# Product-key experts in a two-block transformer: gate products for 128 first indices at once, half of them kept in DRAM

## The chip, the cores and the metric

The kernel runs on one core of a Trainium2 chip. The metric is the device time of one execution in microseconds; the median of three runs of the kernel before is 2450.64 us (2450.23 to 2452.34). A profile of one execution lies beside it.

The engines are called PE (TensorE, with PEld for its weight loads), DVE (VectorE), ACT (ScalarE), POOL (GpSimd) and SP (SyncE, which issues most DMAs).

## The reference, cut to what matters

256 tokens of 1024 channels pass two transformer blocks. The second block has two layers, and each ends with a layer of product-key experts, which is all that the change touches. Its 16384 experts are the pairs of a first and a second index, 128 x 128, and each of 8 heads picks 16 of them per token:

```python
def block(hblk):
    q = (hblk @ wq).reshape(PEER_BLOCK, P_HEADS, 2, D_KEY_HALF)
    s = jnp.einsum('nhpd,hpkd->nhpk', q, keys).astype(jnp.float32)
    top_s, top_i = lax.top_k(s, P_TOPK)
    cand_s = (top_s[:, :, 0, :, None] + top_s[:, :, 1, None, :]).reshape(...)
    cand_i = (top_i[:, :, 0, :, None] * N_KEYS + top_i[:, :, 1, None, :]).reshape(...)
    best_s, best_pos = lax.top_k(cand_s, P_TOPK)
    idx = jnp.take_along_axis(cand_i, best_pos, axis=-1)
    gate = jax.nn.softmax(best_s, axis=-1)
    u = u_tab[idx]
    v = v_tab[idx]
    act = jax.nn.gelu(jnp.einsum('nd,nhkd->nhk', hblk, u))
    return jnp.einsum('nhk,nhkd->nd', (gate * act).astype(v.dtype), v)
```

## The kernel before

The kernel gathers no experts. For each first index e (an "expert tile": the 128 experts that share it) it computes the activations of all 128 experts for all 256 tokens (`a_tile(e)`, a product with the 512 KB tile u[e]) and, later, their part of the output (`v_tile(e)`, with the 512 KB tile v[e]). In between, the activations are multiplied by a dense matrix of gates, which is zero where an expert wasn't picked.

*Tiles of weights.* Every u and v tile is loaded by SP into one of five `raw` buffers and split into two float32r parts (`hilo`, lines 200 to 202): ACT copies the high part `hi` (L201), then DVE, or POOL where the plan says "pool", subtracts to get the low part `lo` (L202). There are three buffers for `hi` and three for `lo`; tile e + 2 is split when tile e is used, so its high part waits until PE has done with tile e - 1. The sets of tiles whose low part POOL computes in the experts are U_POOL0 (five early u tiles), U_POOL (u tiles 65, 71, ..., 107) and V_POOL (v tiles 16, 18, ..., 60).

*Products.* `a_tile` is 24 matmuls with 256 columns (`gemm_t`, L225 to L227), and two tiles share one of the eight PSUM banks; the gelu that reads it into one of eight groups A[0] to A[7] of 16 expert tiles (L1438) follows a tile later. `v_tile` is 12 matmuls with 512 columns (`gemm_n`, L242 to L246) into four banks. Its other operand, the gated activations, is split in two by `w_pair` for two tiles at a time.

*Gates.* `pk16` holds, for every pick (partition) and token, the first index, the second index and the gate in two f16 parts. A gate step handles 8 tokens and 64 of the first indices (c = 0 or 1): `g_hot` makes one-hots of the second index (L1387) and of the first (L1389) on DVE and multiplies the latter by both gate parts (L1392, L1393), `g_mm` does two matmuls of 64 columns a token into one bank (L1401, L1402), and `g_mult` multiplies the activations of four groups in place by them (L1409, four instructions).

*The order* is written out by hand; every engine works through its own queue in that order. `queue_g(c)` queues 34 steps, in step i the matmuls of i - 1, the one-hots of i and the multiplication of i - 2. After each expert tile `fill(budget)` adds a budget to a credit and takes steps off the queue while the credit is positive, a step costing 1.9. Per layer, the experts run so:

```python
        queue_g(0)                     # L1505
        for e in range(64, 112):
            a_tile(e)
            fill(1.4)
        a_flush()
        fill_all()
        acc = [mm([P, 512]) for _ in range(4)]
        for e in range(16):            # v tiles 0 to 15
        for e in range(112, 128):      # u tiles 112 to 127
        queue_g(1)                     # L1519
        for e in range(16, 64):
            v_tile(e, e < 62)
            fill(1.5)
        fill_all()
        for e in range(64, 128):       # v tiles 64 to 127
```

The pool `t4` has four buffers of 4 KB a partition (one-hots, among others; in layer 0 one of them holds a conditioning row all along), `s1` has five of 2 KB.

Of the kernel before, what the change touches and what calls it, by code (L numbers as in the profile page):

```python
# [33 lines left out]
# columns of the packed per-channel vectors  # L34
# [6 lines left out]
# packed constants  # L41
# [7 lines left out]
class _Weights:  # L49
    """The weight tiles in the order of their use: loaded and split into two float32r parts ahead of it."""  # L50
# [30 lines left out]
def _plan(t):  # L81
    """(name, source, engine of the low part) of every weight tile in the order of use"""
# [7 lines left out]
    # the last projection's first tiles go with the second half of the attention heads  # L90
# [31 lines left out]
U_POOL = tuple(range(65, 112, 6))  # L122
V_POOL = tuple(range(16, 62, 2))
# [3 lines left out]
def tile_two_blocks(ctx: ExitStack, tc: tile.TileContext, t: dict, taps=None):  # L127
# [93 lines left out]
    def mm3(out, parts):  # L221
        """out = sum over parts of (stationary hi, lo) x (moving hi, lo), three products each"""
        n = len(parts)
        for i, (sh, sl, mh, ml) in enumerate(parts):
            pe.matmul(out, lhsT=sh, rhs=mh, start=(i == 0), stop=False)  # L225
            pe.matmul(out, lhsT=sh, rhs=ml, start=False, stop=False)  # L226
            pe.matmul(out, lhsT=sl, rhs=mh, start=False, stop=(i == n - 1))  # L227

    def gemm_t(out, w, hT):
        """out [128 cols, 256 tok] from one 128-column weight tile"""  # L230
        wh, wl = [x.rearrange("p (k c) -> p k c", c=P) for x in w]
        mm3(out, [(wh[:, k, :], wl[:, k, :], hT[0][:, k, :], hT[1][:, k, :]) for k in range(KD)])

    def gemm_n(acc, sT, w, first, last, halves=(0, 1)):
        """acc [128 tok, 2, 1024] += rows of one 128-row weight tile"""
# [12 lines left out]
    def ramp(left, tail):  # L248
        """tiles to split ahead when so many are left, this one with them"""
        if tail < TAIL:  # L250
            return LOOK if left > tail else left
        return min(left + NEXT - 1, LOOK + max(0, tail + 4 - left))

    def gemm_rows(acc, sTs, keys, first=True, pumps=0, tail=2):
        """acc += sum of gemm_n over row tiles; returns the last ones, for gemm_tail"""
# [6 lines left out]
    def gemm_tail(acc, tail, hf):  # L262
        """the last row tiles for one half of the tokens, 512 channels at a time"""
# [40 lines left out]
    def ada(w, row, mod, bcol, chunks, group=8, loaded=None, also=None):  # L304
        """mod columns: dot products of the transposed weight rows with silu(c), plus the bias; also: a second row, its
        columns and a scratch"""
# [27 lines left out]
    def row_of(col8):  # L334
        """[128, 8] column layout -> the vector on every partition, by way of DRAM"""
# [8 lines left out]
    def row_pe(col8):  # L344
        """[128, 8] column layout -> the vector on every partition"""
# [19 lines left out]
    def fold(sc, sh, g=None, b=None):  # L365
        """scale, shift columns of modulate(n * g + b): n * (g (1 + sc)) + (b (1 + sc) + sh)"""
# [26 lines left out]
    def T_out(bs, sc, sh, dst, tapname=None, on_vec=(1, 3)):  # L393
        """channel-wise scale and shift on the way to the two float32r parts"""
# [13 lines left out]
    def T_part(bs, fs, q, hf, sc, sh, dst, e1, e2, e3):  # L408
        """half of the tokens of bank q, step by step on the engines given"""
# [14 lines left out]
    def rsqrt(out, var, eps, mul=1.0):  # L424
        """out = (var * mul + eps) ** -0.5"""
# [5 lines left out]
    def rms_scale(chunks):  # L431
        """rsqrt of the mean square over two chunks of 512 channels"""
# [17 lines left out]
    def rms_rows(acc, row, hf):  # L450
        """acc * row, and the scale of its norm"""
# [6 lines left out]
    def rms_residual(yr, X, hf):  # L458
        """X += y * r"""
# [16 lines left out]
    def ln_acc(acc, grow, X, i, stats):  # L476
        """chunk i of X = ALPHA * X + grow * acc, and its statistics"""
# [27 lines left out]
    def T_last(bs, fs, out):  # L505
        """the second half of the tokens, on both engines"""
# [8 lines left out]
    def ln_last(acc, tail, grow, X, n, lgrow, lbrow, store):  # L515
        """X = normalised ALPHA * X + grow * acc, times lgrow, plus lbrow"""
# [31 lines left out]
    def ln_residual(acc, tail, grow, X, n, out, mid=None):  # L548
        """the rest of acc, then n = normalised ALPHA * X + grow * acc; out: scale, shift and where to of n transposed,
        mid(hf): products that need half of that"""  # L550
# [31 lines left out]
    def affine(X, n, lgrow, lbrow, engines):  # L582
        """X = n * g + b"""
# [6 lines left out]
    # =====================================================================================  # L590
    # block 1: windowed attention
    # =====================================================================================
# [4 lines left out]
    xspill = p_dr.tile([NTOK, D], F32, name="xspill")  # L597
    crow = t4()
# [38 lines left out]
    # relative-position bias: bucket table by one-hot product, read back as a Hankel matrix  # L637
# [13 lines left out]
    def kv_prep(k2):  # L651
        """weights, scale and shift of two channel tiles"""
# [52 lines left out]
    # token order of k and v reversed by a permutation product  # L705
# [141 lines left out]
    # =====================================================================================  # L847
    # block 1: feed-forward
    # =====================================================================================
# [53 lines left out]
    # =====================================================================================  # L903
    # block 2, layer 0: differential attention with spatial gate
    # =====================================================================================
# [9 lines left out]
    def rope(o, hf):  # L915
        """rotate [128 tok, 8 x 64]"""
# [54 lines left out]
    def ab_group(gidx, pumps=0, lead=0):  # L971
        """512 output channels of the input projection; keys and values of the context come along, for so many lead
        tiles before the rest"""
# [50 lines left out]
    # concatenated mixer output, transposed: heads 0-3 and the gate, then heads 4-7  # L1024
# [6 lines left out]
    def gate_steps():  # L1031
        """spatial gate, a piece at a time"""
# [196 lines left out]
    # =====================================================================================  # L1229
    # product-key experts  # L1230
    # =====================================================================================
    def peer(li, hT, zacc, mod, before_a, ada_next, after):
# [53 lines left out]
        # views of the scratch that the queries leave  # L1286
# [87 lines left out]
        # gates scattered to [128 second index, 64 first indices] of 8 tokens, times the activations  # L1374
        held = {}

        def g_hot(c, n0):
            sl = slice(n0, n0 + 8)

            def v(q):  # L1380
                return pk16[:, q, sl].rearrange("p (a n) -> p a n", n=4).unsqueeze(2)

            o = t4(2048, F16)
            o2 = o[:, 0:1024].rearrange("p (a i n) -> p a i n", a=2, n=4)
            o1 = o[:, 1024:1536].rearrange("p (a i n) -> p a i n", a=2, n=4)
            oh_ = o[:, 1536:2048].rearrange("p (a i n) -> p a i n", a=2, n=4)
            vec.tensor_tensor(out=o2, in0=v(1).to_broadcast([P, 2, P, 4]),  # L1387
                              in1=iota4.unsqueeze(1).to_broadcast([P, 2, P, 4]), op=OP.is_equal)
            vec.tensor_tensor(out=o1, in0=v(0).to_broadcast([P, 2, 64, 4]),  # L1389
                              in1=iota4[:, c * 64:c * 64 + 64, :].unsqueeze(1).to_broadcast([P, 2, 64, 4]),  # L1390
                              op=OP.is_equal)
            vec.tensor_tensor(out=oh_, in0=o1, in1=v(2).to_broadcast([P, 2, 64, 4]), op=OP.mult)  # L1392
            vec.tensor_tensor(out=o1, in0=o1, in1=v(3).to_broadcast([P, 2, 64, 4]), op=OP.mult)  # L1393
            held["hot", n0] = o2, oh_, o1

        def g_mm(c, n0):
            o2, oh_, ol_ = held.pop(("hot", n0))
            b = mm([P, 8, 64])
            for n in range(8):
                a, m = divmod(n, 4)  # L1400
                pe.matmul(b[:, n, :], lhsT=o2[:, a, :, m], rhs=oh_[:, a, :, m], start=True, stop=False)  # L1401
                pe.matmul(b[:, n, :], lhsT=o2[:, a, :, m], rhs=ol_[:, a, :, m], start=False, stop=True)  # L1402
            held["g", n0] = b

        def g_mult(c, n0):
            b = held.pop(("g", n0))
            for gg in range(4):
                ag = grp(c * 4 + gg)[:, :, n0:n0 + 8]
                vec.scalar_tensor_tensor(out=ag, in0=b[:, :, gg * 16:gg * 16 + 16].rearrange("p n i -> p i n"),  # L1409
                                         scalar=1.0 / GSC, in1=ag, op0=OP.mult, op1=OP.mult)  # L1410

        def queue_g(c):
            def step(i):
                if i >= 1 and i <= 32:
                    g_mm(c, (i - 1) * 8)
                if i < 32:
                    g_hot(c, i * 8)
                if i >= 2:
                    g_mult(c, (i - 2) * 8)

            for i in range(34):
                fill_q.append((1.9, lambda i=i: step(i)))
# [3 lines left out]
        def a_tile(e):  # L1426
            """one expert tile's activations; the nonlinearity follows a tile later"""
# [25 lines left out]
        def v_tile(e, nxt=True):  # L1453
            """one expert tile into the output"""
# [50 lines left out]
        queue_g(0)  # L1505
        for e in range(64, 112):
            a_tile(e)
            fill(1.4)
# [239 lines left out]
```

## Time and profile before

| | |
|---|---|
| median of three runs | 2450.64 us (2450.23 to 2452.34) |
| span of the profiled execution | 2448.3 us |
| PE busy | 2314.1 us (95%) |
| DVE busy | 1878.0 us (77%) |
| ACT busy | 1095.0 us (45%) |
| POOL busy | 472.7 us (19%) |
| HBM read, written | 458.89 MB, 3.19 MB |

Busy times are sums over the whole span, and the span is made of stages with different limits, so what a stage is bound by is read from that stage. Matmuls are pipelined: the duration of one is longer than the distance between the starts of two, and it is the distance that counts. A DVE instruction's duration, too, overlaps the start of the next by some 0.08 us where the next doesn't need its result.

### The profile page before, as it was taken

How to read it: one execution, taken by the hardware profiler on the slowest of the kernel's cores; microseconds unless marked ns; L12 is line 12 of the kernel's file. 1: busy time of each engine (PE TensorE's matmuls, PEld its weight loads, DVE VectorE, ACT ScalarE, POOL GpSimd, SP SyncE). 2: the span in 40 equal slices, each digit the busy share in tenths (PEclk: the TensorE clock that was granted, in tenths of full speed). 3: DMA queues.
4: the chain of work that ended last, by engine and by line, in shares of the span. 5: the costliest groups of instructions: out<-in, count | busy, mean ns of one | idle time of the engine just before them, and what ended most of it. 6: DMA issues, size and time to landing. Idle time of an engine off the chain costs nothing. (4 is left out here: it accounts for less than half of the span.)

```text
span 2448.3 us, 39393 instructions
## 1 busy us (share of the span) xinstructions
PE 2314.1 (95%) x15358; PEld 2043.2 (83%) x15358; DVE 1878.0 (77%) x3510; ACT 1095.0 (45%) x1565; POOL 472.7 (19%) x264
## 2 busy tenths in 40 slices
PE   6888999989998999999999999999999999999998
PEld 4678888867898999988778887898999989777886
DVE  5979868557699678767997778689758754998556
ACT  4653444356554433344334445554443344333443
POOL 3234401021334011002321003243100100332001
PEclk8989999999999999999999999999999999999999
DMA  8666787523455864586446885555654456444664
GB/s 318 206 206 233 242 271 235 199 69 121 158 179 161 282 186 143 151 268 214 130 129 209 294 304 190 190 181 156 181 173 147 147 166 186 131 129 148 196 209 153
DMA packets 129259, 464.66 MB, mean 190 GB/s; under 512 B 14288, under 2 KB 16880, under 8 KB 128944
## 3 DMA queue, kind: packets, MB, share of 16 engines
q1 hardware_dynamic: 129040, 462.11, 59.1%
q8 instruction: 120, 1.97, 0.3%
q14 instruction: 67, 0.55, 0.1%
q10 hardware_dynamic: 32, 0.03, 0.0%
HBM read 458.89 MB, written 3.19 MB: 189 GB/s over the span
## 5 line engine op out<-in xcount | busy, mean ns | idle before, releaser
L201 ACT ACTIVATE hi<-raw 128x1024 fp32r<-128x1024 f32 x668 | 706.1, 1060 | 1036.2 <-PE mm L226 452.5
L202 DVE TENSOR_TENSOR lo<-raw,hi 128x1024 fp32r<-128x1024 f32 x549 | 709.7, 1296 | 397.3 <-ACT hi L201 396.3
L227 PE MATMUL mm<-hTh,lo 128*128 128x256 f32 x2592 | 739.3, 285 | 31.7 <-DVE lo L202 16.5
L225 PE MATMUL mm<-hTh,hi 128*128 128x256 f32 x2592 | 742.4, 286 | 0.7 <-ACT hTh L419 0.7
L226 PE MATMUL mm<-hTl,hi 128*128 128x256 f32 x2592 | 734.4, 283 | 0.2 <-DVE hTl L421 0.2
L202 POOL TENSOR_TENSOR lo<-raw,hi 128x1024 fp32r<-128x1024 f32 x119 | 306.6, 2577 | 1396.1 <-ACT hi L201 1249.5
L227 PEld LDWEIGHTS mm<-hTh,lo 128*128 128x128 f32 x2592 | 497.9, 192 | 40.7 <-DVE lo L202 21.4
L225 PEld LDWEIGHTS mm<-hTh,hi 128*128 128x128 f32 x2592 | 499.4, 193 | 3.8 <-issue 2.6
L226 PEld LDWEIGHTS mm<-hTl,hi 128*128 128x128 f32 x2592 | 498.4, 192 | 0.7 <-POOL hTl L421 0.5
L242 PE MATMUL mm<-hi,s 128*128 128x512 f32 x992 | 315.2, 399 | 4.8 <-ACT s L201 4.8
L244 PE MATMUL mm<-lo,s 128*128 128x512 f32 x992 | 309.5, 394 | 1.1 <-DVE lo L202 1.1
L246 PE MATMUL mm<-hi,s 128*128 128x512 f32 x992 | 308.1, 392 | 0.0
L244 PEld LDWEIGHTS mm<-lo,s 128*128 128x128 f32 x992 | 188.2, 190 | 41.7 <-DVE lo L202 1.5
L246 PEld LDWEIGHTS mm<-hi,s 128*128 128x128 f32 x992 | 188.0, 190 | 40.5 <-DVE s L202 0.3
L242 PEld LDWEIGHTS mm<-hi,s 128*128 128x128 f32 x992 | 184.0, 191 | 40.0 <-ACT s L201 5.6
L1401 PE MATMUL mm<-t 128*128 128x64 f16 x1024 | 143.5, 241 | 18.3 <-DVE t L1392 18.1
L1401 PEld LDWEIGHTS <-t 128*128 128x128 f16 x1024 | 113.9, 117 | 47.6 <-DVE t L1392 27.2
L1402 PE MATMUL mm<-t 128*128 128x64 f16 x1024 | 140.9, 241 | 4.7 <-DVE t L1393 4.6
L202 DVE TENSOR_TENSOR s<-big,s 128x512 fp32r<-128x512 f32 x126 | 117.7, 934 | 16.3 <-ACT s L201 16.3
L1387 DVE TENSOR_TENSOR t<-pk,iota 128x1024 f16<-128x1024 f16 x128 | 120.6, 942 | 0.0
L1402 PEld LDWEIGHTS <-t 128*128 128x128 f16 x1024 | 119.0, 119 | 0.0
L1409 DVE SCALAR_TENSOR_TENSOR big<-mm,big 128x128 f32<-128x128 f32 x512 | 112.3, 282 | 0.0
(283 smaller groups left out, 2763.8 us busy)
## 6 DMA issues: line engine op xcount, KB each, us to landing
raw<-in_u_dram SPq DMA_DIRECT2D x256, 512.0 KB, 3.7
raw<-in_v_dram SPq DMA_DIRECT2D x256, 512.0 KB, 4.2
raw<-in_ada_dram SPq DMA_DIRECT2D x124, 512.0 KB, 4.5
raw<-in_ffn_in_dram SPq DMA_DIRECT2D x44, 512.0 KB, 4.7
raw<-in_ab_in_dram SPq DMA_DIRECT2D x32, 512.0 KB, 5.0
raw<-in_ffn_out_dram SPq DMA_DIRECT2D x22, 512.0 KB, 5.0
big<-in_ada_dram SPq DMA_DIRECT2D x8, 1024.0 KB, 12.9
raw<-in_wn_dram SPq DMA_DIRECT2D x16, 512.0 KB, 5.2
```

Source lines behind the costliest of these rows:

```text
L201: act.activation(out=hi, in_=src, func=AF.Copy)
L202: (eng or vec).tensor_tensor(out=lo, in0=src, in1=hi.bitcast(F32), op=OP.subtract)
L225: pe.matmul(out, lhsT=sh, rhs=mh, start=(i == 0), stop=False)
L226: pe.matmul(out, lhsT=sh, rhs=ml, start=False, stop=False)
L227: pe.matmul(out, lhsT=sl, rhs=mh, start=False, stop=(i == n - 1))
L242: pe.matmul(o[c], lhsT=sh[:, tk], rhs=wh[:, cs[c]], start=first, stop=False)
L244: pe.matmul(o[c], lhsT=sh[:, tk], rhs=wl[:, cs[c]], start=False, stop=False)
L246: pe.matmul(o[c], lhsT=sl[:, tk], rhs=wh[:, cs[c]], start=False, stop=last)
L1387: vec.tensor_tensor(out=o2, in0=v(1).to_broadcast([P, 2, P, 4]), in1=iota4.unsqueeze(1).to_broadcast([P, 2, P, 4]), op=OP.is_equal)
L1401: pe.matmul(b[:, n, :], lhsT=o2[:, a, :, m], rhs=oh_[:, a, :, m], start=True, stop=False)
L1402: pe.matmul(b[:, n, :], lhsT=o2[:, a, :, m], rhs=ol_[:, a, :, m], start=False, stop=True)
L1409: vec.scalar_tensor_tensor(out=ag, in0=b[:, :, gg * 16:gg * 16 + 16].rearrange("p n i -> p i n"), scalar=1.0 / GSC, in1=ag, op0=OP.mult, o ...
```

## The change

The gate products of both halves of the first indices are computed in one go, beside u tiles 64 to 111. A step handles 4 tokens and all 128 first indices. `g_hot(i)` is two DVE instructions: both one-hots in one (1024 f16 elements), then both gate parts times the first (1024 elements). `g_mm` is two matmuls with 128 columns a token, 8 a step. A new `g_out` lets ACT copy the bank to two `s1` buffers, one for each half of the first indices, 4 tokens a step. After every second step, the first half (8 tokens) is multiplied into the activations (`g_times`, from SBUF now), and the second half is written to a DRAM tile `gspill` by a DMA that ACT issues. 67 steps are queued at 1.9, and the budget of these u tiles is 2.75 instead of 1.4.

Beside v tiles 16 to 63, `queue_g1` queues 17 steps at 1.5 with a budget of 0.65: each reads 16 tokens of `gspill` back into a `t4` buffer (512 KB, issued by SP) and multiplies the ones read a step earlier into the activations. No matmul and no one-hot is left there.

U_POOL and V_POOL are empty, so DVE computes those low parts. U_POOL0 stays. Comments and docstrings that the diff also takes out are not shown.

```diff
-U_POOL = tuple(range(65, 112, 6))
-V_POOL = tuple(range(16, 62, 2))
+U_POOL = ()
+V_POOL = ()
...
+    gspill = p_dr.tile([P, NTOK, 64], F32, name="gspill")
...
-        def g_hot(c, n0):
-            sl = slice(n0, n0 + 8)
-
-            def v(q):
-                return pk16[:, q, sl].rearrange("p (a n) -> p a n", n=4).unsqueeze(2)
-
-            o = t4(2048, F16)
-            o2 = o[:, 0:1024].rearrange("p (a i n) -> p a i n", a=2, n=4)
-            o1 = o[:, 1024:1536].rearrange("p (a i n) -> p a i n", a=2, n=4)
-            oh_ = o[:, 1536:2048].rearrange("p (a i n) -> p a i n", a=2, n=4)
-            vec.tensor_tensor(out=o2, in0=v(1).to_broadcast([P, 2, P, 4]),
+        def g_hot(i):
+            sl = slice(i * 4, i * 4 + 4)
+            o = t4(2048, F16).rearrange("p (q i n) -> p q i n", i=P, n=4)
+            vec.tensor_tensor(out=o[:, 0:2], in0=pk16[:, 0:2, sl].unsqueeze(2).to_broadcast([P, 2, P, 4]),
                               in1=iota4.unsqueeze(1).to_broadcast([P, 2, P, 4]), op=OP.is_equal)
...
+            vec.tensor_tensor(out=o[:, 2:4], in0=o[:, 0].unsqueeze(1).to_broadcast([P, 2, P, 4]),
+                              in1=pk16[:, 2:4, sl].unsqueeze(2).to_broadcast([P, 2, P, 4]), op=OP.mult)
+            held["hot", i] = o
+
+        def g_mm(i):
+            o = held.pop(("hot", i))
+            b = mm([P, 4, P])
+            for n in range(4):
+                pe.matmul(b[:, n, :], lhsT=o[:, 1, :, n], rhs=o[:, 2, :, n], start=True, stop=False)
+                pe.matmul(b[:, n, :], lhsT=o[:, 1, :, n], rhs=o[:, 3, :, n], start=False, stop=True)
+            held["g", i] = b
+
+        def g_out(i):
+            b = held.pop(("g", i))
+            if i % 2 == 0:
+                held["gs"] = [s1(512).rearrange("p (n i) -> p n i", i=64) for _ in range(2)]
+            for c in range(2):
+                act.activation(out=held["gs"][c][:, i % 2 * 4:i % 2 * 4 + 4, :], in_=b[:, :, c * 64:c * 64 + 64],
+                               func=AF.Copy, scale=1.0 / GSC)
+            if i % 2 == 1:
+                gs = held.pop("gs")
+                held["g0", i // 2] = gs[0]
+                adma(out=gspill[:, i * 4 - 4:i * 4 + 4, :], in_=gs[1])
+
+        def g_times(g, c, n0, n):
             for gg in range(4):
-                ag = grp(c * 4 + gg)[:, :, n0:n0 + 8]
-                vec.scalar_tensor_tensor(out=ag, in0=b[:, :, gg * 16:gg * 16 + 16].rearrange("p n i -> p i n"),
-                                         scalar=1.0 / GSC, in1=ag, op0=OP.mult, op1=OP.mult)
+                ag = grp(c * 4 + gg)[:, :, n0:n0 + n]
+                vec.tensor_tensor(out=ag, in0=g[:, :, gg * 16:gg * 16 + 16].rearrange("p n i -> p i n"), in1=ag,
+                                  op=OP.mult)
 
+        def queue_g0():
             def step(i):
+                if i < 64:
+                    g_hot(i)
+                if 1 <= i <= 64:
+                    g_mm(i - 1)
+                if 2 <= i <= 65:
+                    g_out(i - 2)
+                if i >= 4 and i % 2 == 0:
+                    g_times(held.pop(("g0", i // 2 - 2)), 0, i * 4 - 16, 8)
 
+            for i in range(67):
                 fill_q.append((1.9, lambda i=i: step(i)))
 
+        def queue_g1():
+            def step(i):
+                if i < 16:
+                    held["g1", i] = t4().rearrange("p (n i) -> p n i", i=64)
+                    dma(out=held["g1", i], in_=gspill[:, i * 16:i * 16 + 16, :])
+                if i >= 1:
+                    g_times(held.pop(("g1", i - 1)), 1, i * 16 - 16, 16)
+
+            for i in range(17):
+                fill_q.append((1.5, lambda i=i: step(i)))
...
-        queue_g(0)
+        queue_g0()
         for e in range(64, 112):
             a_tile(e)
-            fill(1.4)
+            fill(2.75)
...
-        queue_g(1)
+        queue_g1()
         for e in range(16, 64):
             v_tile(e, e < 62)
-            fill(1.5)
+            fill(0.65)
```

## Rows read from the trace of the kernel before

**Rows 1.** First part of the page: busy us (share of the span), instructions.
```profile
PE 2314.1 (95%) x15358; PEld 2043.2 (83%) x15358; DVE 1878.0 (77%) x3510; ACT 1095.0 (45%) x1565; POOL 472.7 (19%) x264
```

**Rows 2.** Windows of five stages: length, busy per engine, granted clock, DMA share, GB/s.
```profile
869.10:1040.90 171.80, 171.80 (x1667) 170.22 (x1665) 135.25 (x297) 62.65 (x72) 17.75 (x8) 1.00 0.50 151
1815.30:1987.10 171.80, 171.75 (x1666) 170.17 (x1664) 135.28 (x297) 62.68 (x73) 17.68 (x8) 1.00 0.50 148
1133.20:1317.60 184.40, 173.34 (x1089) 140.30 (x1090) 170.22 (x307) 63.31 (x72) 55.70 (x22) 0.97 0.47 140
2079.30:2263.00 183.70, 171.70 (x1088) 139.05 (x1089) 170.92 (x307) 63.38 (x72) 55.86 (x22) 0.98 0.45 137
1317.60:1450.00 132.40, 132.40 (x586) 109.54 (x585) 101.66 (x125) 64.93 (x75) 0.00 (x0) 1.00 0.87 292
```

**Rows 3.** Timeline of PE in U: start us, us, engine, line, operation.
```profile
878.78 0.28 PE L227 MATMUL mm<-hTh,lo 128*128 128x256 f32 x1
878.90 0.23 PE L1401 MATMUL mm<-t 128*128 128x64 f16 x1
878.95 0.23 PE L1402 MATMUL mm<-t 128*128 128x64 f16 x1
...
879.81 0.24 PE L1402 MATMUL mm<-t 128*128 128x64 f16 x1
879.86 0.36 PE L225 MATMUL mm<-hTh,hi 128*128 128x256 f32 x1
880.06 0.28 PE L226 MATMUL mm<-hTl,hi 128*128 128x256 f32 x1
880.18 0.28 PE L227 MATMUL mm<-hTh,lo 128*128 128x256 f32 x1
```

**Rows 4.** Timeline of PE among v tiles, one tile apart.
```profile
1320.32 0.62 PE L242 MATMUL mm<-hi,s 128*128 128x512 f32 x2
...
1323.04 0.62 PE L242 MATMUL mm<-hi,s 128*128 128x512 f32 x2
```

**Rows 5.** Timeline of DVE and POOL in V of layer 0.
```profile
1162.96 1.22 DVE L202 TENSOR_TENSOR lo<-raw,hi 128x1024 fp32r<-128x1024 f32 x1
...
1164.09 0.69 DVE L1387 TENSOR_TENSOR t<-pk,iota 128x1024 f16<-128x1024 f16 x1
1164.12 2.91 POOL L202 TENSOR_TENSOR lo<-raw,hi 128x1024 fp32r<-128x1024 f32 x1 [5.86 <-ACT hi L201]
...
1164.69 2.62 DVE L1389 TENSOR_TENSOR t<-pk,iota 128x512 f16<-128x512 f16 x1
...
1169.54 0.68 DVE L1387 TENSOR_TENSOR t<-pk,iota 128x1024 f16<-128x1024 f16 x1
...
1170.14 0.42 DVE L1389 TENSOR_TENSOR t<-pk,iota 128x512 f16<-128x512 f16 x1
...
1171.39 0.88 DVE L1409 SCALAR_TENSOR_TENSOR big<-mm,big 128x128 f32<-128x128 f32 x4
...
1172.19 1.22 DVE L202 TENSOR_TENSOR lo<-raw,hi 128x1024 fp32r<-128x1024 f32 x1
```

**Rows 6.** Waits in V of layer 0: total us, times, longest us.
```profile
PE mm L1401 <- DVE t L1392: 8.6, 9, 1.3
```

**Rows 7.** ACT's copy of 256 elements from PSUM; its one DMA issue; DMA landings.
```profile
L870 ACT ACTIVATE s<-mm 128x256 f32<-128x256 f32 x22 | 8.0, 363 | 0.0
...
L684 ACTq DMA_DIRECT2D btab<-t x1: 353/353/353, 28.0 to 28.0; - x1
...
btab<-t ACTq DMA_DIRECT2D x1, 32.0 KB, 4.4
...
raw<-in_v_dram SPq DMA_DIRECT2D x256, 512.0 KB, 4.2
```

**Rows 8.** Two of the one-hot lines on DVE: ns min/median/max.
```profile
L1387 DVE TENSOR_TENSOR t<-pk,iota x128: 676/685/2903, 871.5 to 2238.9; 128x1024 f16<-128x1024 f16 x128
...
L1392 DVE TENSOR_TENSOR t<-t,pk x128: 424/425/2516, 872.6 to 2242.2; 128x512 f16<-128x512 f16 x128
```

More of the change, by code (lines that the diff above doesn't have):

```diff
@@ L1375, in peer @@
         held = {}
-        def g_hot(c, n0):
-            sl = slice(n0, n0 + 8)
-            def v(q):
-                return pk16[:, q, sl].rearrange("p (a n) -> p a n", n=4).unsqueeze(2)
-            o = t4(2048, F16)
-            o2 = o[:, 0:1024].rearrange("p (a i n) -> p a i n", a=2, n=4)
-            o1 = o[:, 1024:1536].rearrange("p (a i n) -> p a i n", a=2, n=4)
-            oh_ = o[:, 1536:2048].rearrange("p (a i n) -> p a i n", a=2, n=4)
-            vec.tensor_tensor(out=o2, in0=v(1).to_broadcast([P, 2, P, 4]),
-                              in1=iota4.unsqueeze(1).to_broadcast([P, 2, P, 4]), op=OP.is_equal)
[L1389 to L1406, printed above, removed]
+        def g_hot(i):
+            sl = slice(i * 4, i * 4 + 4)
+            o = t4(2048, F16).rearrange("p (q i n) -> p q i n", i=P, n=4)
+            vec.tensor_tensor(out=o[:, 0:2], in0=pk16[:, 0:2, sl].unsqueeze(2).to_broadcast([P, 2, P, 4]),
+                              in1=iota4.unsqueeze(1).to_broadcast([P, 2, P, 4]), op=OP.is_equal)
+            vec.tensor_tensor(out=o[:, 2:4], in0=o[:, 0].unsqueeze(1).to_broadcast([P, 2, P, 4]),
+                              in1=pk16[:, 2:4, sl].unsqueeze(2).to_broadcast([P, 2, P, 4]), op=OP.mult)
+            held["hot", i] = o
@@ L1407, in g_mult @@
+        def g_times(g, c, n0, n):
             for gg in range(4):
-                ag = grp(c * 4 + gg)[:, :, n0:n0 + 8]
-                vec.scalar_tensor_tensor(out=ag, in0=b[:, :, gg * 16:gg * 16 + 16].rearrange("p n i -> p i n"),
-                                         scalar=1.0 / GSC, in1=ag, op0=OP.mult, op1=OP.mult)
-        def queue_g(c):
+                ag = grp(c * 4 + gg)[:, :, n0:n0 + n]
+                vec.tensor_tensor(out=ag, in0=g[:, :, gg * 16:gg * 16 + 16].rearrange("p n i -> p i n"), in1=ag,
+                                  op=OP.mult)
@@ L1413, in step @@
+        def queue_g0():
             def step(i):
[L1414 to L1421, printed above, removed]
-                fill_q.append((1.9, lambda i=i: step(i)))
+                if i < 64:
[7 more added lines that the diff above has]
+            for i in range(67):
+                fill_q.append((1.9, lambda i=i: step(i)))
```

## Prediction

> **What bounds the kernel now.** The page's first part is read first: TensorE (PE) is busy 95% of the span, VectorE (DVE) 77%, GpSimd (POOL) 19% [rows 1]. An average doesn't say which of them ends a wait, so the span is cut at the stages that the change touches [rows 2]. "U" is here the 48 expert tiles e = 64 to 111 with the gate steps of queue_g(0) between them, "V" the 48 tiles e = 16 to 63 of the output with those of queue_g(1); each comes once in each of the two layers. In U (171.8 us, twice) PE is busy all the time and DVE 135 us: PE is the bound. In V (184.4 and 183.7 us) DVE is busy 170 us, PE has gaps, its clock's granted mean is 0.97 and 0.98, and POOL is busy 56 us. The fifth row, V tiles of the same kind without gate steps (e = 64 and up, layer 0), has PE busy for the whole window, clock 1.00, although the transfers run at 292 GB/s and DVE is busy 102 of 132 us.
>
> What a gate step costs PE is read from the timeline: its 16 matmuls of 64 columns start 0.061 us apart, and from its first to the point where the tile's 0.12 us beat is back it takes 880.06 - 0.12 - 878.90 = 1.04 us [rows 3]. So U is 32 x 1.04 = 33.3 us of gates and 138.5 us of tiles, 2.885 us each, which is 24 x 0.12. A V tile is 2.72 us, 0.227 us for each of its 12 matmuls [rows 4]. V without any wait would be 48 x 2.72 + 33.3 = 163.9; some 20 us of it are lost to DVE. The cause is seen in the timeline: when POOL takes a low part (L202, 2.91 us), the DVE operation beside it, normally 0.42 us, takes 2.62 [rows 5]. The matmuls of the gate step then wait for that DVE work, up to 1.3 us at a time [rows 6].
>
> **The change, part by part.** Per layer, always against the profiled execution (span 2448.3; the median of the runs is 2.3 us more, so differences are simply carried to the median).
>
> *V loses its gate products.* 512 matmuls, 32 x 1.04 us, go, and with them every wait of PE on the one-hots; the 23 POOL splits go too, so nothing stretches DVE. What remains are tiles at PE's own beat: 48 x 2.72 = 130.6, say 131 with a little for the seams. This saves 53.4 us in layer 0 and 52.7 in layer 1, together 106.1. The cover: DVE takes all 48 splits and the reread products, 16 x 4 multiplies of 256 elements at no more than twice the 0.20 us from start to start of today's 128 [rows 5], 25.6 us. The fifth of rows 2 carries as many splits and 25 conditioning products beside them within 102 us, so DVE fits. Transfers: 512 KB every 2.72 us is 193 GB/s; the read-back is 512 KB every 1.5/0.65 = 2.3 tiles, 83 GB/s more; 276 together, below the 292 at which PE had no gap. SP issues the reads between those of V. Behind a read that waits for its t buffer would stand V's loads, and behind those ACT's and DVE's splits; but the buffer was freed two steps (4.6 tiles, 12 us) before, the write landed a stage earlier, and five raw buffers lie ahead against a landing of 4.2 us [rows 7]. I cost it at nothing; if that cover failed, PE would wait for V.
>
> *U takes all the gate products.* 64 steps of 8 matmuls with 128 columns. No row shows f16 at 128 columns. Below, it can't beat the 0.061 us that 64 columns need; above, 64 further columns at the streaming price (0.227 - 0.120)/256 = 0.00042 us a column give 0.061 + 0.027 = 0.088. The line through 256 and 512 columns gives 0.067, and since the 64-column beat lies well above that line (0.040), something else than streaming sets it, which 128 columns may hide behind: I take 0.067. A step is 8 x 0.067 + 0.06 for the seam = 0.60, 64 of them 38.2, so PE needs 138.5 + 38.2 = 176.7 us, 5 more than now.
>
> The Trainium skill, page "TensorE: Matmul & The Clock Gate", section "Back-to-back issue gap", says that a sustained stream of weight loads and matmuls needs about 81 ns a pair at 128 columns; by that estimate 512 pairs take 41.5 us instead of 34.3 and the forecast would be 14 us later, at 2380. The same place gives about 131 ns at 512 columns, where rows 4 have 227, so this stream doesn't follow its figures, and the sum goes without it.
>
> *DVE in U.* Start to start: a low part 1.13 us; a one-hot of 1024 elements 0.60; four multiplies 0.80 [rows 5]. The new second operation multiplies 1024 f16 elements and needs the first one's result: between 0.69 (the one-hot of the same size and pattern) and 0.85 (two of L1392's 0.425) [rows 8]. I take 0.69, with the same access pattern: a step is 1.30, all in all 48 x 1.13 + 64 x 1.30 + 32 x 0.80 = 163 us, at the upper end 176. So DVE is nearly as full as PE, where now it has 36 us to spare.
>
> *ACT in U.* To the 62.7 us of rows 2 come 128 copies of 256 elements from PSUM at 0.363 and 32 DMA issues at 0.353 [rows 7]: 120 us. That isn't the bound, but it waits in order: the copy-out of a step waits for that step's matmuls, and behind it stands the high part of tile e + 3, behind that DVE's low part. With fill(2.75) against 1.9 a step, fills hold alternately two steps and one; now there is never a second. I walk two tiles, time 0 at the end of tile e - 1: matmuls of one step to 0.6, tile e to 3.5, two steps' matmuls to 4.7, tile e + 1 to 7.6. ACT's high part of e + 2 ends at 1.3, DVE's low part at 2.5, the one-hots that the second group of matmuls needs at 3.8: PE wants them at 4.1, 0.3 later. ACT copies the first of the two steps out at 4.3 and comes to the high part of e + 3 at 5.1 to 5.4, 2 us after its buffer was free; DVE is through at 5.9 and waits for it until 6.4. It then does low part, one-hots and, in every second round, one set of multiplies more, and ends at 9.7, 0.9 late. The next double step then waits some 0.5 us on PE. That is 0.5 us in four tiles, 11 or 12 times: 6 us. U becomes 176.7 + 6 = 182.7, 10.9 more than now, 21.8 for both layers. The write of 256 KB every two steps is some 50 GB/s beside 138 of U; rows 2 show the core at 292.
>
> *U without POOL splits*: DVE was no bound there, so taking the 8 stretches away gains nothing by itself.
>
> Sum: 2450.6 - 106.1 + 21.8 = 2366.3.
>
> **The rivals.**
> A. DVE becomes the bound in U. For it: 163 to 176 us of work against PE's 176.7, and the forced wait of 0.5 us in two tiles, 12 us in a stage. Against it: a late DVE swallows that wait. With the multiply at its upper end, 176 + 12 + the ends, U is some 195, 12 more per layer: 2391.
> B. V doesn't run at PE's beat, since the read-back holds up V's loads. For it: 276 GB/s is near the most that rows 2 show with PE full, and SP is in order. At a tenth more, 144 us, it is 2392. Against it: the fifth of rows 2.
> C. Slower than before: the write issued by ACT holds ACT until it has landed, not only for its issue. The one DMA that ACT issues now takes 0.353 us to issue and 4.4 to land [rows 7]. With x us per write ACT needs 109 + 32x; it begins to bind above 2.3 us and eats up the whole gain of 42 us a layer above 3.6; at 4.4 U is 250 and the time 2366 + 2 x 67 = 2500. Against it: 0.353.
> That the steps might not fit the tiles and run on into a stage without cover is excluded by the code: 67 x 1.9 = 127 is below 48 x 2.75 = 132, 17 x 1.5 = 25.5 below 48 x 0.65 = 31.
>
> **How the numbers follow.** Forecast 0.66, A 0.18, B 0.08, C 0.05; 0.03 is left for a loss that I don't see. The range: below, 0.061 us a matmul and no wait give U 174, 2.2 us more per layer: 2349. Above, 0.088 with the 6 us of waits gives U 193.5 and 2388; DVE's upper end with a heavier wait gives 199 and 2399; a little of B on top, 2402. It takes in A and B. Measurements of this kernel tell 0.2%, 5 us, from no change: faster is the forecast, A and B, 0.92; slower C and some of the rest, 0.06; in between 0.02.
>
> **What would show it.** V: 131 us, PE busy throughout, clock 1.00, no DVE operation over 2 us beside it; transfers near 276 GB/s. U: 177 to 187 us, gate matmuls 0.062 to 0.07 us apart, PE's only waits those of the second gate group on DVE's multiply, ACT near 120 us, DVE 160 to 180. Rival A shows as PE waiting for one-hots after most tiles and DVE busy without idle time; B as ACT's high part waiting for the DMA of V; C as long gaps on ACT behind its DMA. A gate matmul of 0.088 us or more, or a multiply of more than 0.85, makes the time wrong, not the sign.

## The result

The changed kernel takes 2398.54 us (median of four runs, 2398.1 to 2399.53), beside 2450.77 for the kernel before: a ratio of 0.9782, 95% interval 0.9768 to 0.9795. It is faster and inside the range of 2349 to 2402, but 32.5 us later than the forecast of 2366: of the 84 us that the sum promised, 52 came.

### The profile page after: what moved, and what is told of

It reads as the page before. It is cut to its first block, busy times and chain, and to the rows that moved or that the text cites. A ratio compares the mean times of both kernels' runs of the same rounds, so it can differ in the third digit from the quotient of the medians.

```text
span 2396.2 us, 37336 instructions
## 1 busy us (share of the span) xinstructions
PE 2284.1 (95%) x14334; PEld 2029.0 (85%) x14334; DVE 1838.3 (77%) x3188; ACT 1170.7 (49%) x1821; POOL 315.5 (13%) x202
## 5 line engine op out<-in xcount | busy, mean ns | idle before, releaser
L202 DVE TENSOR_TENSOR lo<-raw,hi 128x1024 fp32r<-128x1024 f32 x611 | 784.5, 1287 | 402.4 <-ACT hi L201 400.6
L242 PE MATMUL mm<-hi,s 128*128 128x512 f32 x992 | 306.1, 390 | 4.8 <-ACT s L201 4.8
L246 PE MATMUL mm<-hi,s 128*128 128x512 f32 x992 | 305.4, 389 | 0.0
L202 POOL TENSOR_TENSOR lo<-raw,hi 128x1024 fp32r<-128x1024 f32 x57 | 151.1, 2653 | 1008.5 <-ACT hi L201 979.3
L242 PEld LDWEIGHTS mm<-hi,s 128*128 128x128 f32 x992 | 185.8, 188 | 44.1 <-ACT s L201 5.6
L1401 ACT ACTIVATE s<-mm 128x256 f32<-128x256 f32 x256 | 84.1, 384 | 120.6 <-PE mm L1393 120.4
L1392 PE MATMUL mm<-t 128*128 128x128 f16 x512 | 126.0, 295 | 1.5 <-DVE t L1384 1.5
L1393 PE MATMUL mm<-t 128*128 128x128 f16 x512 | 126.9, 297 | 0.0
L429 POOL TENSOR_TENSOR sm<-sm,mhalf 128x1 f32<-128x1 f32 (+1 forms) x18 | 11.5, 640 | 780.0 <-DVE sm L428 779.9
L320 DVE SCALAR_TENSOR_TENSOR raw<-raw,t 128x1024 f32<-128x1024 f32 x84 | 104.6, 1247 | 4.8 <-DMA raw<-in_ada_dram 4.8
L1384 DVE TENSOR_TENSOR t<-t,pk 128x1024 f16<-128x1024 f16 x128 | 88.6, 692 | 4.4
L202 DVE TENSOR_TENSOR s<-big,s 128x512 fp32r<-128x512 f32 x126 | 86.3, 685 | 6.2 <-ACT s L201 6.2
```

The lines of the kernel that those rows point to most:

```text
L202: (eng or vec).tensor_tensor(out=lo, in0=src, in1=hi.bitcast(F32), op=OP.subtract)
L242: pe.matmul(o[c], lhsT=sh[:, tk], rhs=wh[:, cs[c]], start=first, stop=False)
L246: pe.matmul(o[c], lhsT=sl[:, tk], rhs=wh[:, cs[c]], start=False, stop=last)
L320: vec.scalar_tensor_tensor(out=o, in0=r, scalar=1.0, in1=c, op0=OP.mult, op1=OP.mult, accum_out=m[:, j:j + 1])
L1384: vec.tensor_tensor(out=o[:, 2:4], in0=o[:, 0].unsqueeze(1).to_broadcast([P, 2, P, 4]), in1=pk16[:, 2:4, sl].unsqueeze(2).to_broadcast([P, ...
L1392: pe.matmul(b[:, n, :], lhsT=o[:, 1, :, n], rhs=o[:, 2, :, n], start=True, stop=False)
```

## The profile after

The first part of the page answers rows 1. PE has 14334 matmuls instead of 15358, yet only 30 us less busy time; POOL has lost 157 us.

```profile
PE 2284.1 (95%) x14334; PEld 2029.0 (85%) x14334; DVE 1838.3 (77%) x3188; ACT 1170.7 (49%) x1821; POOL 315.5 (13%) x202
```

The windows of the stages, as in [rows 2]: U of both layers, then V of both.

```profile
868.40:1068.60 200.20, 199.46 (x1666) 195.04 (x1664) 178.28 (x306) 100.21 (x200) 0.00 (x0) 1.00 0.52 171
1788.00:1988.10 200.10, 199.36 (x1666) 195.01 (x1664) 177.54 (x304) 100.23 (x200) 0.00 (x0) 1.00 0.52 169
1161.00:1291.65 130.65, 130.65 (x576) 108.18 (x577) 105.99 (x137) 63.26 (x72) 0.00 (x0) 1.00 0.78 260
2080.40:2211.12 130.72, 130.67 (x576) 108.25 (x577) 106.05 (x137) 63.34 (x72) 0.00 (x0) 1.00 0.75 252
```

V is at PE's own beat, 130.7 us, with 576 matmuls and no gap: 106.7 us saved in the two layers, where the sum had 106.1. U is 200.2 and 200.1 us instead of 171.8: 56.7 us lost, where the sum had 21.8. The whole miss lies in U. The timeline of PE there (as [rows 3]) shows what a gate step costs now.

```profile
876.02 0.28 PE L1392 MATMUL mm<-t 128*128 128x128 f16 x1
876.13 0.30 PE L1393 MATMUL mm<-t 128*128 128x128 f16 x1
876.25 0.30 PE L1392 MATMUL mm<-t 128*128 128x128 f16 x1
...
876.84 0.30 PE L1393 MATMUL mm<-t 128*128 128x128 f16 x1
876.88 0.37 PE L225 MATMUL mm<-hTh,hi 128*128 128x256 f32 x1
877.09 0.28 PE L226 MATMUL mm<-hTl,hi 128*128 128x256 f32 x1
```

The eight matmuls start 0.117 us apart, not 0.067, and the step takes 877.09 - 0.12 - 876.02 = 0.95 us, not 0.60. The other new work, in the same order as in the prediction: the wait of PE for one-hots in U of layer 0 (from the list of waits: total, times, longest), the multiplication of the activations there (group of DVE: busy, mean ns) and the DMA that ACT issues, with its issue in ns and its landing.

```profile
PE mm L1392 <- DVE t L1384: 0.7, 1, 0.7
...
L1411 DVE TENSOR_TENSOR big<-s,big 128x128 f32<-128x128 f32 x128 | 40.4, 378 | 0.0
...
L1406 ACTq DMA_DIRECT2D gspill<-s x64: 326/326/351, 878.2 to 1980.3; - x64
...
gspill<-s ACTq DMA_DIRECT2D x64, 256.0 KB, 2.0
```

## The experiments

**What sets the distance of the gate matmuls.** Both operands of a gate matmul are f16 tiles with the token innermost, four tokens together, so PE reads one element in four, 8 bytes apart. That is so in both kernels. Theory 1 is that the step of the moving operand halves the rate at which its columns stream. Then 64 columns were streaming, too, at 0.00092 us a column, and 128 cost twice as much. Theory 2 blames the weight load, which has the same step; theory 3 blames DVE.

*moving_adjacent.*

```diff
+            f = o.rearrange("p q i n -> p q (i n)")
-  pe.matmul(..., rhs=o[:, 2, :, n], ...)                  # and o[:, 3, :, n]
+  pe.matmul(..., rhs=f[:, 2, n * P:n * P + P], ...)       # and f[:, 3, ...]
```

> The changed kernel, but the moving operand of the gate matmuls is read as 128 adjacent f16 elements instead of one element in four; the weights are still read one in four. The gates come out wrong, all the work stays. Theory 1 (the step of the moving operand halves the rate at which columns stream: 0.118 us for 128 columns, 0.061 for 64, so 0.00092 us a column): the gate matmuls start 0.056 to 0.068 us apart, U needs 138.5 + 64 x (8 x 0.062 + 0.08) = 175 us on PE and, with DVE now as full as PE, 176 to 184 instead of 200; the time falls from 2398 to 2350 to 2368. Theory 2 (the weight load, whose step is the same, sets the distance): 0.118 us still, U 200, time 2396 to 2401. Theory 3 (the loss in U is DVE's, the distance only follows it): U stays near 200 even where the distance falls.

Measured: 2367.78 us, ratio to the kernel before 0.9655 (95% interval 0.9639 to 0.9671). The timeline of PE, then the windows of U in both layers, then the wait for one-hots in layer 0:

```profile
879.16 0.22 PE L1394 MATMUL mm<-t 128*128 128x128 f16 x1
879.22 0.22 PE L1393 MATMUL mm<-t 128*128 128x128 f16 x1
...
879.49 0.22 PE L1394 MATMUL mm<-t 128*128 128x128 f16 x1
...
871.90:1055.40 183.50, 173.83 (x1666) 168.99 (x1664) 175.88 (x306) 99.14 (x200) 0.00 (x0) 1.00 0.58 188
1774.50:1958.00 183.50, 173.85 (x1666) 169.03 (x1665) 175.20 (x304) 99.16 (x200) 0.00 (x0) 1.00 0.57 184
...
PE mm L1393 <- DVE t L1384: 9.7, 12, 1.2
```

The distance is 0.055 us and U 183.5, as theory 1 expects. DVE does the same work as in the changed kernel, so theory 3 falls. PE is busy 173.8 us and idle 9.7, all of it waiting for one-hots, 12 times.

*weights_adjacent.*

```diff
-  pe.matmul(..., lhsT=o[:, 1, :, n], ...)
+  pe.matmul(..., lhsT=f[:, 1, n * P:n * P + P], ...)      # f as above, in both matmuls
```

> The changed kernel, but the stationary operand of the gate matmuls is read as 128 adjacent f16 elements; the moving one is still read one in four. The gates come out wrong, all the work stays. Theory 1 (step of the moving operand): distance 0.118 us as before, U 200, time within 3 us of 2398. Theory 2 (weight load): distance 0.06, U 176 to 184, time 2350 to 2368.

Measured: 2394.61 us in one run. Timeline of PE and window of U:

```profile
875.59 0.30 PE L1394 MATMUL mm<-t 128*128 128x128 f16 x1
875.71 0.29 PE L1393 MATMUL mm<-t 128*128 128x128 f16 x1
...
867.90:1066.90 199.00, 198.25 (x1666) 194.07 (x1664) 177.92 (x306) 99.96 (x200) 0.00 (x0) 1.00 0.53 172
```

The distance stays at 0.116 to 0.117 us and U at 199.0; the time is a little below the expected 2395 to 2401. Theory 2 falls.

*before_moving_adjacent.* The same edit in the kernel before.

```diff
-  pe.matmul(..., rhs=oh_[:, a, :, m], ...)                # and ol_[:, a, :, m]
+  pe.matmul(..., rhs=fh[:, a, m * 64:m * 64 + 64], ...)   # and fl[...]; oh_ and ol_ as flat rows
```

> The kernel before, but the moving operand of its gate matmuls is read as 64 adjacent elements; the gates come out wrong, all the work stays. Theory 1 in the form that the 64-column distance of 0.061 us was already streaming at 0.00092 us a column: the distance falls, to 0.03 to 0.055 us; U, where PE is the bound, falls from 171.8 by 512 x 0.006 to 0.03, to 156 to 169 us. The premise of the forecast (something else than streaming sets the 64-column distance): 0.061 stays and U stays at 171 to 172.

Measured: 2424.89 us in one run. Timeline of PE, then the windows of U and V in layer 0, then the wait for one-hots in that V:

```profile
875.50 0.20 PE L1402 MATMUL mm<-t 128*128 128x64 f16 x1
875.53 0.20 PE L1403 MATMUL mm<-t 128*128 128x64 f16 x1
...
867.80:1028.10 160.30, 160.30 (x1681) 158.77 (x1679) 142.94 (x297) 62.64 (x73) 19.85 (x8) 1.00 0.54 166
1120.40:1306.18 185.78, 164.36 (x1088) 129.93 (x1089) 173.51 (x307) 63.28 (x72) 57.98 (x22) 0.95 0.46 139
...
PE mm L1402 <- DVE t L1392: 18.2, 12, 2.0
```

0.033 us instead of 0.061: at 64 columns, too, it is the step of the moving operand that sets the distance of [rows 3]. U falls to 160.3. V doesn't fall, 185.8 us beside 184.4, though its gate matmuls take half the time: PE waits the longer for DVE's one-hots, 18.2 us instead of 8.6 [rows 6].

*moving_step16.* One element in eight.

```diff
-  pe.matmul(..., rhs=o[:, 2, :, n], ...)                  # and o[:, 3, :, n]
+  pe.matmul(..., rhs=f[:, :, n], ...)                     # and f[:, :, 4 + n]; f: o[:, 2:4] as 128 rows of 8
```

> The changed kernel with the moving operand of the gate matmuls read one element in eight, 16 bytes apart, instead of 8. The gates come out wrong, all the work stays. If the columns come at a fixed number of bytes swept per second (0.118 us for 128 columns at 8 bytes), 16 bytes make it 0.23 to 0.24 us: U is 138.5 + 64 x (8 x 0.236 + 0.08) = 264 us and the time some 2527. If any step of 8 bytes or more runs at one reduced rate, 0.118 us, U 200 and a time within 3 us of 2398.

Measured: 2545.78 us in one run. Timeline of PE and three windows: the tile that follows the first eight gate matmuls, the next gate step, and U as a whole:

```profile
878.61 0.40 PE L1393 MATMUL mm<-t 128*128 128x128 f16 x1
878.83 0.41 PE L1394 MATMUL mm<-t 128*128 128x128 f16 x1
879.06 0.41 PE L1393 MATMUL mm<-t 128*128 128x128 f16 x1
...
874.20:877.40 3.20, 3.20 (x17) 3.18 (x16) 1.93 (x3) 0.66 (x2) 0.00 (x0) 0.51 0.43 152
...
878.60:880.30 1.70, 1.70 (x11) 0.93 (x9) 0.52 (x1) 1.54 (x2) 0.00 (x0) 1.00 0.00 0
868.00:1145.90 277.90, 277.16 (x1671) 222.94 (x1669) 179.86 (x307) 102.06 (x200) 0.00 (x0) 0.91 0.40 125
```

0.23 us at a granted clock of 1.00, as a fixed number of bytes swept per second expects: 128 columns 16 bytes apart are 2048 bytes in 0.23 us, 8 bytes apart 1024 in 0.117, 8.9 and 8.8 bytes per ns. U is 277.9 us instead of 264; in that stage the granted clock is 0.91, which the expectation hadn't reckoned with.

*pairs.* The one-hots for two tokens together, so that both operands lie 4 bytes apart. The gates stay right; DVE needs one instruction more a step. (`pk16` is interleaved to match, and the matmuls' indices follow; neither is shown.)

```diff
-            o = t4(2048, F16).rearrange("p (q i n) -> p q i n", i=P, n=4)
+            o = t4(2048, F16).rearrange("p (q i n) -> p q i n", i=P, n=2)
...
+            for a in range(2):     # instead of one multiply
+                vec.tensor_tensor(out=o[:, 4 + 2 * a:6 + 2 * a], in0=o[:, 2 * a]..., in1=pg[:, 2 * i + a]..., op=OP.mult)
```

> The changed kernel with the one-hots laid out for pairs of tokens instead of fours, so that both operands of the gate matmuls are read one element in two (4 bytes apart instead of 8). The multiply on DVE becomes two of 512 elements, 0.2 us more a step. Theory 1 in its narrow form (4 bytes apart is as fast as the f32 operands, which lie 4 bytes apart too): distance 0.056 to 0.068 us; PE needs 175 us in U, DVE 48 x 1.13 + 64 x 1.50 + 32 x 1.2 = 189, so U is 187 to 195 and the time 2372 to 2390. Theory 1 in its wide form (any step above 2 bytes costs it): distance 0.118, U 200 to 206, time 2396 to 2412. Theory 2 predicts the same as the narrow form.

Measured: 2373.38 us, ratio 0.9675 (0.9659 to 0.9691). Timeline of PE and window of U:

```profile
877.92 0.22 PE L1400 MATMUL mm<-t 128*128 128x128 f16 x1
877.98 0.22 PE L1399 MATMUL mm<-t 128*128 128x128 f16 x1
...
870.80:1057.80 187.00, 175.23 (x1666) 169.12 (x1665) 180.20 (x370) 99.21 (x200) 0.00 (x0) 1.00 0.57 183
```

0.058 us at 4 bytes: the narrow form of theory 1. These 512 bytes in 0.058 us are again 8.8 bytes per ns; adjacent elements, 256 bytes in 0.055 us, are only 4.7, so below 4 bytes a column something else sets the price, some 0.00043 us a column. DVE is now the fuller engine in U (180 of 187 us), which is rival A in a kernel where PE is no longer slow.

**What made V long.** The prediction put two causes together: POOL stretching DVE's operations, and gate matmuls that wait for DVE. Each of the two halves of the change was tried alone.

*before_no_pool.* Only U_POOL and V_POOL emptied, in the kernel before.

> The kernel before with U_POOL and V_POOL empty, so that DVE computes these low parts, and nothing else changed. If V was long because POOL stretched DVE's operations by some 2.1 us each, DVE has 170 - 23 x 2.1 + 23 x 1.13 = 148 us, and V falls from 184 to PE's own 164 to 170 with the gate products still in it; U stays at 172 to 174; time 2412 to 2426. If DVE was full with its own work, V stays above 178 us and the time above 2438.

Measured: 2413.63 us, ratio 0.9836 (0.9819 to 0.9852), beside 2453.81 for the kernel before, run with it.

*pool_back.* Only U_POOL and V_POOL as they were, in the changed kernel.

> The changed kernel with the 8 + 23 low parts per layer back on POOL (U_POOL and V_POOL as in the kernel before). If POOL's stretching of DVE was only harmful because the gate matmuls waited for DVE, little is lost: in V DVE has 106 us - 23 x 1.13 + 23 x 2.1 = 128 of 131, V 131 to 138; in U 178 - 8 x 1.13 + 8 x 2.1 = 186 of 200, U 200 to 203; time 2398 to 2418. If POOL's splits were themselves what made V long, whatever stands beside them, V goes back to 150 us or more and the time to 2437 or more.

Measured: 2415.43 us, ratio 0.9843 (0.9826 to 0.9859), beside the same 2453.81. The window of V in layer 0 and the one-hots of the second index (ns min/median/max) of before_no_pool; then, of pool_back, the window of V, the largest wait of PE in it (total us, times, longest) and DVE's low parts in it:

```profile
1133.50:1298.89 165.39, 165.37 (x1088) 136.14 (x1089) 152.95 (x329) 63.39 (x72) 0.00 (x0) 1.00 0.52 155
...
L1387 DVE TENSOR_TENSOR t<-pk,iota x128: 682/684/690, 871.8 to 2202.1; 128x1024 f16<-128x1024 f16 x128
```

```profile
1163.90:1300.64 136.74, 131.87 (x576) 107.86 (x577) 123.25 (x115) 63.31 (x72) 58.25 (x22) 1.00 0.76 249
...
PE mm L244 <- DVE lo L202: 4.9, 3, 1.8
...
L202 DVE TENSOR_TENSOR lo<-raw,hi x26: 1206/1214/3387, 1168.1 to 1299.2; 128x1024 fp32r<-128x1024 f32 x26
```

Without POOL's splits V is 165.4 us with its gate products, PE busy throughout, and DVE's busy time falls from 170 to 153 although it does 23 splits more: the longest of its one-hots takes 0.69 us, where it took 2.9 [rows 8]. Of the 19.0 us by which V was longer in the kernel before, PE stood idle for 11.1 [rows 2]; the rest it spent busy, at a granted clock of 0.97 that is 1.00 here. The gate products on PE are worth the rest of V, 165.4 - 130.7 = 34.7. But in U they cost 28.5 again, so once the sets are empty their move brings some 6 us a layer.

Yet the emptied sets aren't the larger part of the change. Each half alone brings about as much: the emptied sets 40.2 us (2453.81 to 2413.63), the move 38.4 (2453.81 to 2415.43). Together they bring 52.2 and not the sum of 79, since each takes most of the same loss out of V. In pool_back no gate matmul is left in V to wait for DVE, and POOL's splits still cost 6 us there and 2 in U: in V PE waits for DVE's low parts, of which the longest takes 3.4 us where 1.2 is usual.

**A version that is faster than both.** *pairs_turned* goes on from pairs: ACT writes the copied-out gates with the token innermost, so that DVE's multiplications read adjacent elements.

```diff
+                gv = held["gs"][c].rearrange("p (i n) -> p n i", n=8)[:, i % 2 * 4:i % 2 * 4 + 4, :]
-                act.activation(out=held["gs"][c][:, i % 2 * 4:i % 2 * 4 + 4, :], in_=...)
+                act.activation(out=gv, in_=...)
...
-   in0=g[:, :, gg * 16:gg * 16 + 16].rearrange("p n i -> p i n")
+   in0=g[:, gg * 128:gg * 128 + 128].rearrange("p (i n) -> p i n", n=8)
```

> The kernel of the run pairs, with ACT writing the gates token-innermost, so that the multiplications of the activations read them in adjacent elements instead of 256 bytes apart (128 elements each, in V twice as many of them). If the step makes them take 377 ns instead of the 282 that the same multiplication took from PSUM, they come back to some 280 ns and 0.20 us from start to start, DVE has 180 - 32 x 0.36 = 168 us in U and falls below PE's 175: U 179 to 184 instead of 187, time 2358 to 2368. If reading gates from SBUF costs that by itself, 377 ns and U 187 stay, time 2371 to 2376.

Measured: 2361.43 us, ratio 0.9621 (0.9605 to 0.9638). Its window of U, two waits in it, and the two lines that changed their price (min/median/max in ns):

```profile
869.00:1050.40 181.40, 173.42 (x1666) 168.92 (x1664) 169.58 (x370) 128.63 (x200) 0.00 (x0) 1.00 0.59 188
...
DVE lo L202 <- ACT hi L201: 8.9, 11, 3.3
...
PE mm L1399 <- DVE t L1390: 5.7, 9, 1.2
...
L1419 DVE TENSOR_TENSOR big<-s,big x256: 282/285/292, 881.1 to 1947.3; 128x128 f32<-128x128 f32 x128
...
L1409 ACT ACTIVATE s<-mm x256: 630/686/792, 873.3 to 1943.3; 128x256 f32<-128x256 f32 x128
```

The multiplication takes 285 ns again instead of 375 in pairs; ACT's copy pays for it, 686 ns instead of 378, but ACT has the room (129 of 181 us). U is 181.4.

## Why the prediction was right, and where it was not

**V: right, term and mechanism.** 130.7 us against 131, clock 1.00, no gap on PE, transfers at 252 and 260 GB/s against the forecast 276. Rival B is out: the read-back costs nothing that shows. That the waits for DVE made V long was right as well; before_moving_adjacent shows it from one side (half the gate time, no gain) and before_no_pool from the other: with the gate products and without POOL's splits V is 165.4 us, where the prediction had 163.9 without any wait, and U is 171.6, so that emptying U_POOL gains nothing there. What the prediction didn't ask is how much each half of the change does alone.

**U: one term was mis-sized.** The step that failed is the price of a 128-column gate matmul. The text put it between 0.061 and 0.088 us and took 0.067; it is 0.117. The upper bound, 0.088, added 64 columns at the price of the f32 operands, 0.00042 us each, and the choice inside rested on a guess: since 64 columns lay above the line through 256 and 512, "something else than streaming sets it, which 128 columns may hide behind". There was nothing to hide behind. The f16 columns streamed at 0.0009 us each since they lie 8 bytes apart, which the access pattern in the code said and the text didn't weigh; the nearest rows in number of columns were not the nearest in layout. The plain doubling, 0.122, would have been the bound to set. Per layer this is 64 x (0.95 - 0.60) = 22.4 us. With its own upper bound for the matmul the prediction came to 2388; that 2398.5 is still in the range is luck, since the range reached on to 2402 only for a fuller DVE that bounds U and for rival B, and neither set the time.

**The waits in U: the walk was right in number, roughly in size.** It gave 11 or 12 waits of PE, 6 us per layer. With the slow matmuls DVE had time and PE waited 0.7 us, so 5.3 us came back. Where the matmuls are fast, PE waits 12 times for 9.7 us (moving_adjacent, DVE busy 175.9 us instead of the forecast 163) and idles 8.0 us (pairs_turned, DVE busy 169.6). The step on which the walk builds, DVE waiting for a high part from ACT, shows 11 times in pairs_turned, but only 4 times (4.8 us) in moving_adjacent, where DVE is nearly full with its own work. That the forecast lies close to moving_adjacent, 182.7 us for U against 183.5 and 2366 against 2367.8, is partly luck: PE's own time is 3 us below the 176.7 of the sum there, and its waits are 4 above the 6. 22.4 - 5.3 = 17.1 us a layer, 34 in all, less some 2 us gained outside the two stages, where nobody looked for the cause, is the miss of 32.5.

**DVE and ACT in U:** the one-hots and the wide multiply were priced right (0.685 and 0.692 us; a step takes 1.33 from start to start, forecast 1.30). The multiplications were not: 0.30 us from start to start, not 0.20, since their gates lie 256 bytes apart in SBUF; pairs_turned shows that the step is the cause. In the kernel before they lay 256 bytes apart as well, but in PSUM, and a multiplication took 282 ns. The 128 of them make 12.8 of the 15 us by which DVE's 178.3 exceed the forecast 163. It didn't show in the result since PE was slower still. (The upper end of 176 is a slip: 48 x 1.13 + 64 x 1.45 + 32 x 0.80 is 173.) ACT's copies were priced a little high: ACT is busy 100.2 us, where the sum without the DMA issues, which the profile doesn't count, has 109.

**Rivals.** A, DVE as the bound of U, gave the time that came (2391 against 2398.5) but not the mechanism: DVE is idle 22 of 200 us and PE waits 0.7. C is out: ACT's DMA holds it 0.326 us, though it takes 2.0 to land.

**The cited price** that the prediction set aside, 81 ns a pair at 128 columns (the Trainium skill, page "TensorE: Matmul & The Clock Gate", section "Back-to-back issue gap"), fits neither layout here: 55 ns with adjacent elements, 117 with elements 8 bytes apart. What bears on the step is the Trainium skill, page "SBUF — State Buffer", section "Door 1: The DMA port swizzle (why `[64,N]` ≈ `[32,N]`)": it says that consecutive accesses keep full bandwidth as long as at least two fall into the same 16-byte line. By that a step of 8 bytes, two accesses a line, would be free; the runs show half the rate there, and the measurement decides.

## What to carry to other kernels

A matmul's price is taken from rows with the same layout of the moving operand, not only the same number of columns; where two sizes of it can't be compared, the plain proportional price belongs among the bounds. Joining small matmuls into fewer wide ones saves little when columns, not instructions, are what is paid for: the gate matmuls of 8 tokens take 2 x 0.95 us on PE now and took 2 x 1.04. Where an engine helps another out, look at what its help does to that engine's other operations: taking the help away, and nothing else, gave 40 us here. And where a change has two halves, try each alone before the gain is shared out: these two overlap, and either gives some three quarters of it.

## What the runs showed of the hardware

- f16 columns of the moving operand: 128 of them every 0.055 us adjacent, 0.058 at 4 bytes, 0.117 at 8 and 0.23 at 16. From 4 bytes on that is 8.8 to 8.9 bytes swept per ns. The step of the weights made no difference that matters (0.116 to 0.117).
- A DVE multiplication of 128 f32 elements took 285 ns with adjacent elements of its first operand in SBUF and 375 with elements 256 bytes apart (pairs_turned and pairs). An ACT copy of 256 elements from PSUM took 378 ns into adjacent elements and 686 into elements 32 bytes apart.
- Beside a POOL low part a DVE operation of 0.42 us took 2.62 [rows 5]; with those POOL operations gone, the longest one-hot fell from 2.9 to 0.69 us (before_no_pool).
- In moving_step16 the granted clock was 0.51, the lower of the two levels (1.2 GHz) for most of that window, during the tile that followed a first burst of slow gate matmuls, and 0.91 over U, although PE counted as busy for 277 of 278 us. In moving_adjacent, whose PE was idle for 9.7 us in U, it was 1.00. PE had waited 0.74 us just before that first burst; but from 900 to 920 us the granted clock was 0.88 with PE counted as busy all the time. What it is about the slow matmuls that lowers it wasn't tried.
